# Two thirds of the chunk MLP's u products by seven block products, modulation chapters moved, output parts held behind the next operand's transposes

## The chip, the cores and the metric

The kernel runs on one core of one Trainium2 chip. The metric is the device time of one execution in microseconds (us). TensorE (PE) does the matrix products, VectorE (DVE) and ScalarE (ACT) the elementwise work, GpSimd (POOL) a few small steps, and SyncE (SP) issues nearly all the DMA loads. Each of these engines works through its own list of instructions strictly in the order of that list; an instruction that waits holds up all that stand behind it on its engine.

## The reference

Two layers work on a latent stream x (512 tokens of 1024 channels) and a context (256 tokens). Each layer is a half-step SwiGLU, a token mixer and another SwiGLU; every sub-layer is modulated and post-normalised. Layer 0 mixes with a bidirectional HGRN2, layer 1 with a chunk MLP:

```python
def modulation(cond, w_mod, b_mod):
    m = jax.nn.silu(cond) @ w_mod + b_mod            # nine "chapters" of 1024 per layer
    return m.reshape(m.shape[:-1] + (N_MOD, D_MODEL))
def modulate(x, m, k):
    return x * (1 + m[..., 3 * k + 1, :]) + m[..., 3 * k, :]
def post_norm_update(x, y, m, k, g, b):
    return layer_norm(DN_ALPHA * x + m[..., 3 * k + 2, :] * y, g, b)
def swiglu(h, w_in, w_out):
    gate, up = jnp.split(h @ w_in, 2, axis=-1)
    return (jax.nn.silu(gate) * up) @ w_out           # hidden width 2816
def chunk_mlp(h, n_chunks, w_in, v_g, v_b, w_s, b_s, w_out):
    u, v = jnp.split(jax.nn.gelu(h @ w_in), 2, axis=-1)   # each 3072 wide
    v = layer_norm(v, v_g, v_b)
    v = v.reshape(bsz, n_chunks, CM_CHUNK, CM_GROUPS, CM_INNER // CM_GROUPS)
    v = jnp.einsum('gts,bnsgc->bntgc', w_s, v) + b_s.T[None, None, :, :, None]
    return (u * v.reshape(bsz, length, CM_INNER)) @ w_out
```

So chapters 3k and 3k+1 of a layer (shift and scale) are needed when the operand of sub-layer k is made, and chapter 3k+2 (the gate) when its output is added to x. For layer 1, chapters 6 and 7 belong to the last SwiGLU's input, and chapter 8 is the gate on its output.

## The kernel before, in words

**Precision.** Every large product is made of three fp32r matmuls (lines 148, 149, 150) of operands that are split into a high part (ACT, line 135) and the rest (DVE, line 136). A stationary block is 128x128, a moving block 128 rows by up to 512 tokens.

**Stages on PE.** The first SwiGLU of the latent and context tokens, HGRN2, then f2 (the last SwiGLU of layer 0, up to 1340 us of the profiled execution), f3 (the first of layer 1, up to 1695 us), the chunk MLP and f4, the last SwiGLU. Each SwiGLU has an input phase and an output phase.

**Input phase by seven products (class FeedSums, used by f2, f3 and f4).** The first hidden pairs are made plainly while the operand is still being built (banks named psf); all others come as a gate block and an up block whose 2x2 block product takes seven products of half-size blocks rather than eight: 84 matmuls of 128x256 in banks psc, pse and psa. For that, DVE forms sums of the weights for each pair (lines 594 to 597, from tiles raw and rawu), ACT and DVE split the sums into w, and DVE combines the products (lines 666 to 671). Sums of the operand (f4 to f7) are made once per phase.

**Output phase (class OutPhase).** For each of two column halves, hidden blocks (hs, split from h by lines 135 and 136) are multiplied into four token banks y0 to y3. The last steps of the second half are "held": they run token by token, so that a finished token can be added to x with its gate (line 350), normalised (lines 360 to 374), transposed on PE (pt, line 384) and scaled into the next phase's operand xm while PE still works on later tokens. `run` begins with `self.load_gate(0)`, which loads the gate's row. `finish` scales the residual x by the affine vectors of the norm (lines 343 and 344).

**Chunk MLP.** The v half comes by seven products already, in pairs. The u half is 24 plain units: 24 matmuls of 128x512 per unit into pscu, gelu on ACT (line 1329), then eight short matmuls that mix tokens (pscs, line 1334), then DVE (lines 1341, 1345, 1350). Before the first unit DVE and POOL make the mean and 1/deviation of v (lines 1297 to 1301), and DVE normalises v with them (line 1318).

**Modulation.** One chapter is a queue of nine steps. Eight of them load 512 KB of mod_w and take two dot products of 128x512 on DVE (line 170); the ninth closes the chapter. For a gate chapter the close is a reduction, an addition, a transpose on PE, a copy and a DMA to memory:

```python
nc.vector.reduce_sum(dot, accs[c], axis=AX.X)
if ch % 3 == 2:
    nc.vector.tensor_tensor(dot, dot, mbT[:, l, ch, :], ALU.add)
    pg = bank("pg")
    nc.tensor.transpose(pg[:KD, :P], dot, ident)
```

Other code calls `mod_step(n)` to move the queue on by n steps. `made(key)` runs the queue until that chapter is closed; `load_gate` calls it for the gate:

```python
self.gate = load_row(self.bp, "rgate", made((self.l, 3 * self.j + 2, self.cond))[0, c])
```

In the kernel before, chapters 7, 6 and 8 of layer 1 are queued just ahead of the u stage, are stepped by `mod_step(2)` once in each unit, and are closed well before its end. `Scraps` is a pool that makes the small tiles of a chapter out of one larger tile and takes its weight buffers from the two-buffer ring rawu that the seven products use too.

**What sets the order.** The program text is the order, except where `issue_after` gives work a lower priority: a scheduler then places it among the other work of its engine.

Of the kernel before, what the change touches and what calls it, by code (L numbers as in the profile page):

```python
# [18 lines left out]
P = 128  # L19
# [51 lines left out]
def backbone_kernel(  # L71
# [126 lines left out]
    class Scraps:  # L198


        def __init__(self, pool, small, ring):
            self.pool, self.ring, self.at, self.got = pool, ring, 0, {}
            self.small = pool.tile([P, D], F32, tag=small, name=small, bufs=2)

        def tile(self, shape, dtype, tag, name, bufs=1):
            if tag == "mraw":
                return self.pool.tile(shape, dtype, tag=self.ring, name=self.ring, bufs=2)
            got = self.got.setdefault(tag, [0])
            if got[0] < bufs and tag != "junk" or len(got) == 1:
                got.append(self.at)  # L210
                self.at += int(np.prod(shape[1:]))
                assert self.at <= D
            a = got[1 + got[0] % (len(got) - 1)]
            got[0] += 1
            t = self.small[: shape[0], a : a + int(np.prod(shape[1:]))]
            return t.rearrange("p (k i) -> p k i", i=shape[2]) if len(shape) > 2 else t

    def scraps(sp, l, chs):

        s = sp.tile([P, D], F32, tag="e", name="e", bufs=2)  # L220
# [49 lines left out]
    class OutPhase:  # L270
# [128 lines left out]
        def run(self, bp, hook=None, nmod=0):  # L399
# [27 lines left out]
            self.held.close()  # L427
            if self.release:
                self.release()
            if nxt is not None:  # L430
                nxt.enter()
# [5 lines left out]

            if nxt is None:
                done(0)
                done(1)  # L440
                return
# [157 lines left out]
    class FeedSums(Forms, FeedIn):  # L599


        def __init__(self, l, i, xm, nt, new_block):
            super().__init__(l, i, xm, nt)
            self.place_forms(new_block)

        def rest(self, hp, sp, nmod=0):
            for f in range(len(self.pss) // 2):
# [835 lines left out]
```

## Time and profile before

| | |
|---|---|
| time, median of 3 | 2471.17 us (2470.74 to 2472.19) |
| the profiled execution's own time | 2472.61 us |
| its span on the core | 2470.9 us |
| busy in it: PE, DVE, ACT, POOL | 2426.5, 1919.2, 1133.4, 45.5 us |
| mean granted TensorE clock | 0.996 |

The places that the change touches, by the start of their first PE instruction in the profiled execution:

| us | what starts |
|---|---|
| 984.26, 1340.68, 1694.91, 2108.53 | transposes of the new operand for f2, f3, the chunk MLP, f4 |
| 1017.44, 1371.05, 2138.93 | first pair by seven products of f2, f3, f4 |
| 1822.96 to 1977.06 | u stage of the chunk MLP |
| 1988.75 | main part of its output phase |
| 2341.03 | output phase of f4, the last phase |

Times in the profile are microseconds from the start of the span, means of a group are nanoseconds. A busy interval of a PE row lasts longer than the distance to the next row, since matmuls are pipelined, so PE's pace is read from starts. A row of the windows view gives the stretch, its length, the busy time and number of instructions in it, the granted clock, the DMA share and GB/s.

### The profile page before, as it was taken

Reading aid. Unit: us, or ns where it says so; the run is one execution under the profiler, and the core shown is the slowest. Engines: PE = TensorE matmul, PEld = TensorE weight load, DVE = VectorE, ACT = ScalarE, POOL = GpSimd, SP = SyncE. Lnnn points to the kernel's source line nnn. Section 1 sums busy time; section 2 is a strip of 40 time slices with the busy share of each in tenths; the row PEclk is TensorE's granted clock in tenths of the full one; section 3 lists DMA queues with packets and bytes.
Section 4 is the critical chain, followed back from the end, with each engine's and each line's share of the span. In section 5 each row is a group of like instructions: output and inputs, shape, how many; then the busy total and the mean of one; then the engine's idle time right before and its main releaser. Section 6 shows DMA issues by size and latency. Waiting matters only on the chain.

```text
span 2470.9 us, 37394 instructions
## 1 busy us (share of the span) xinstructions
PE 2426.5 (98%) x14619; PEld 2181.9 (88%) x14619; DVE 1919.2 (78%) x3426; ACT 1133.4 (46%) x1726; POOL 45.5 (2%) x83
## 2 busy tenths in 40 slices
PE   7999999999999999999999999999999999999998
PEld 5888889987888888999988999988988888999986
DVE  7965679685588886998886988887889466998765
ACT  4222344453454552655643555544652243555641
POOL 0000000000000000000000000000000000000001
PEclk9999999999999999999999999999999999999999
DMA  8866555874211214332463333673356243332332
GB/s 318 297 204 200 166 196 186 287 250 139 69 60 52 60 52 159 111 128 104 151 216 129 111 104 109 205 221 129 103 186 221 86 149 115 128 125 103 103 113 71
DMA packets 106851, 365.45 MB, mean 148 GB/s; under 512 B 12409, under 2 KB 13617, under 8 KB 106673
## 3 DMA queue, kind: packets, MB, share of 16 engines
q1 hardware_dynamic: 106672, 363.06, 44.3%
q8 instruction: 114, 1.87, 0.3%
q14 instruction: 65, 0.52, 0.1%
HBM read 350.40 MB, written 12.61 MB: 147 GB/s over the span
## 4 chain that ended last, share of the span: by engine, by line
PE 83%; DVE 11%; ACT 2%; issue 2%; DMA 1%; POOL 1%; SPq 0%; POOLq 0%; DVEq 0%; ACTq 0%
PE y L150 8%; PE y L149 8%; PE y L148 8%; PE psf L149 6%; PE psf L150 6%; PE psf L148 6%; PE psc L148 5%; PE psc L150 5%; PE psc L149 5%; PE pse L148 2%; PE pse L150 2%; PE pse L149 2%; PE pscu L148 2%; PE pscu L149 2%; PE pscu L150 2%
## 5 line engine op out<-in xcount | busy, mean ns | idle before, releaser
L136 DVE TENSOR_TENSOR w<-raw,w 128x1024 fp32r<-128x1024 f32 (+2 forms) x446 | 505.3, 1136 | 150.6 <-ACT w L135 149.6
L135 ACT ACTIVATE w<-raw 128x1024 fp32r<-128x1024 f32 (+2 forms) x446 | 439.5, 987 | 352.5 <-PE y L150 91.7
L150 PE MATMUL y<-w,hs 128*128 128x512 f32 x984 | 383.3, 390 | 0.8 <-DVE hs L136 0.8
L148 PE MATMUL y<-w,hs 128*128 128x512 f32 x984 | 383.4, 390 | 0.6 <-ACT hs L135 0.6
L149 PE MATMUL y<-w,hs 128*128 128x512 f32 x984 | 382.9, 389 | 0.0
L135 ACT ACTIVATE hs<-h 128x512 fp32r<-128x512 f32 (+1 forms) x220 | 127.2, 588 | 232.5 <-PE y L150 216.7
L150 PEld LDWEIGHTS y<-w,hs 128*128 128x128 f32 x984 | 184.7, 188 | 40.7 <-DVE hs L136 2.5
L148 PEld LDWEIGHTS y<-w,hs 128*128 128x128 f32 x984 | 184.7, 188 | 39.4 <-ACT hs L135 1.0
L149 PEld LDWEIGHTS y<-w,hs 128*128 128x128 f32 x984 | 184.7, 188 | 38.3
L148 PE MATMUL psf<-xm,w 128*128 128x512 f32 (+1 forms) x544 | 192.9, 361 | 17.5 <-ACT xm L135 17.2
L136 DVE TENSOR_TENSOR hs<-h,hs 128x512 fp32r<-128x512 f32 (+1 forms) x220 | 135.6, 634 | 93.7 <-ACT hs L135 93.6
L150 PE MATMUL psf<-xm,w 128*128 128x512 f32 (+1 forms) x544 | 194.2, 358 | 2.3 <-DVE w L136 2.3
L149 PE MATMUL psf<-xm,w 128*128 128x512 f32 (+1 forms) x544 | 194.5, 358 | 0.7 <-DVE xm L136 0.5
L148 PE MATMUL pse<-f,w 128*128 128x256 f32 x480 | 136.2, 284 | 3.3 <-ACT w L135 3.3
L148 PE MATMUL psc<-f,w 128*128 128x256 f32 x480 | 136.1, 284 | 0.0
L148 PE MATMUL psc<-xm,w 128*128 128x256 f32 x480 | 135.9, 283 | 0.0
L150 PE MATMUL pse<-f,w 128*128 128x256 f32 x480 | 135.9, 283 | 0.0
L149 PE MATMUL pse<-f,w 128*128 128x256 f32 x480 | 135.8, 283 | 0.0
L149 PE MATMUL psc<-xm,w 128*128 128x256 f32 x480 | 135.8, 283 | 0.0
L149 PE MATMUL psc<-f,w 128*128 128x256 f32 x480 | 135.8, 283 | 0.0
L150 PE MATMUL psc<-f,w 128*128 128x256 f32 x480 | 135.8, 283 | 0.0
L150 PE MATMUL psc<-xm,w 128*128 128x256 f32 x480 | 135.8, 283 | 0.0
(314 smaller groups left out, 6006.3 us busy)
## 6 DMA issues: line engine op xcount, KB each, us to landing
raw<-in_ffn_w_in SPq DMA_DIRECT2D x160, 512.0 KB, 4.4
raw<-in_ffn_w_out SPq DMA_DIRECT2D x110, 512.0 KB, 4.0
mraw<-in_mod_w SPq DMA_DIRECT2D x104, 512.0 KB, 4.3
rawu<-in_ffn_w_in SPq DMA_DIRECT2D x60, 512.0 KB, 3.5
rawu<-in_mod_w SPq DMA_DIRECT2D x40, 512.0 KB, 4.4
x<-x SPq DMA_DIRECT2D x36, 512.0 KB, 4.2
raw<-in_hg_wf SPq DMA_DIRECT2D x32, 512.0 KB, 3.5
raw<-in_cm_wu SPq DMA_DIRECT2D x24, 512.0 KB, 4.0
```

The source lines that it names most:

```text
L135: nc.scalar.activation(dst_hi, src, AF.Copy)
L136: latest[0] = nc.vector.tensor_tensor(dst_lo, src, dst_hi.bitcast(F32), ALU.subtract)
L148: nc.tensor.matmul(ps, ah, bh, start=start, stop=False, **kw)
L149: nc.tensor.matmul(ps, ah, bl, start=False, stop=False, **kw)
L150: return nc.tensor.matmul(ps, al, bh, start=False, stop=stop, **kw)
```

## The change

1. In the u stage, `seven` (moved out of FeedSums into a class that both users share) makes two units together by seven products, for 16 of the 24 units; the other 8 stay plain. The units are taken in pairs, the operand's sums stay until the last pair, and DVE normalises each group of v just ahead of its use.
2. Chapters 7 and 6 move from the u stage into the chunk MLP's output phase, one step per loop step. Chapter 8 moves to the last phase: it is queued by `scraps(sp, 1, (8,))` just ahead of `op.run`.
3. In an output phase that leads into another phase and has more than two blocks of tokens (the five that end at about 380, 984, 1341, 1695 and 2109 us), the last token's last two held steps (12 matmuls) are issued behind the transposes of the first two blocks of the next operand. What followed the held parts moves with them, and the second pair of tokens is staged into psf one block later.
4. In the first pair of FeedSums, one product (psa) comes right behind the first one, and the last product gets a bank of its own (psb).
5. The scaling of x in `finish` is given a lower priority.

```diff
-    def scraps(sp, l, chs):
+    def scraps(sp, l, chs, small=None):
...
-        small = Scraps(sp, "e", "rawu")
+        small = Scraps(sp, small, "rawu")
...
-                for x in self.xs:
-                    nc.vector.scalar_tensor_tensor(x[:, c], x[:, c], ALPHA, g, ALU.mult, ALU.mult)
-                    nc.vector.scalar_tensor_tensor(x[:, c], b, ALPHA, x[:, c], ALU.mult, ALU.add)
+                with tc.issue_after(latest[0].ins):
+                    for x in self.xs:
+                        nc.vector.scalar_tensor_tensor(x[:, c], x[:, c], ALPHA, g, ALU.mult, ALU.mult)
+                        nc.vector.scalar_tensor_tensor(x[:, c], b, ALPHA, x[:, c], ALU.mult, ALU.add)
...
+            back = 2 if nxt is not None and nt > 2 else 0
+            rest = [(1, *h, [nt - 1]) for h in held[len(held) - back :]]
             for t in range(nt):
-                for h in held:
+                for h in held[: len(held) - back * (t == nt - 1)]:
                     self.part(1, *h, [t])
...
             for i in range(len(steps) + 3):
-                if i == 1 and nt > 2:
-                    done(1)
+                if i == back:
+                    for r in rest:
+                        self.part(*r)
+                    close()
+                    nxt.enter()
+                    if nt > 2:
+                        done(1)
                 if i:
                     nxt.ahead(i)
+                if back and i == 4:
+                    nxt.staged(*steps[1])
                 if i < len(steps):
-                    last = self.operand(*steps[i])
-                if i >= 3:
-                    nxt.staged(*steps[i - 3])
+                    self.operand(*steps[i])
+                j = i - 2 if back and i > 3 else i - 3
+                if 0 <= j < len(steps):
+                    nxt.staged(*steps[j])
...
+            product(pc, wg, 0, b11, True, True)
+            kept(0, pc)
+            if early:
                 product(pa, wg, K2, b21, True, True)
+            product(pe, we, 0, self.f5, True, True)
...
-            modp = early.enter_context(swap("modp3"))
-            srow = {"x": silu_row(modp, "x")}
-            for ch in (7, 6, 8):
-                queue_mod(modp, srow, 1, ch, ["x"])
...
+            def by_sums(j):
+                u0, u1 = (cu.tile([P, T], F32, tag="u", name="u", bufs=4) for _ in range(2))
+                sc = cu.tile([P, 2 * P], F32, tag="sc3", name="sc3", bufs=1)
+                lo, hi = slice(0, 2 * P), slice(2 * P, T)
+                pa, pe, pc, _ = gin.seven(xm, sp, cm_wu[j], cm_wu[j + 1], [u0[:, lo], u1[:, hi], u1[:, lo], sc])
...
+            for j in range(0, 3 * NG, 2):
+                for i in (j, j + 1):
+                    if i % 3 == 0:
+                        normalize(i // 3)
+                        hs.append(vhp.tile([P, 3, T], F32, tag="vh", name="ht"))
+                if j % 6 < 4:
+                    us = by_sums(j)
+                else:
+                    us = plain(j), plain(j + 1)
...
-                    mod_step(2)
...
-        op.run(bp)
+        small = vhp.tile([P, NT, GC], F32, tag="vh", name="vt").rearrange("p t c -> p (t c)")
+        scraps(modp, 1, (7, 6), small)
+        op.run(bp, None, 1)
...
         op.affine = (1, 1)
-        op.run(bp)
+        scraps(sp, 1, (8,))
+        op.run(bp, None, 1)
```

How the instructions move at three places. First, PE at the passage from the chunk MLP's output phase to f4, before and then now. y3 is the last token's bank, pt the transposes of the new operand's blocks from the normalised x of the first tokens, psf the first plain product of f4; each y3 row stands for itself and the two rows of its three matmuls that are left out.

```order
L148 MATMUL y3_19472<-w_19801,hs_19807 128x512
...
L148 MATMUL y3_19472<-w_19812,hs_19815 128x512
...
L148 MATMUL y3_19472<-w_19812,hs_19818 128x512
...
L384 MATMUL pt_19947<-ident_74,x_19065 128x128
...
L384 MATMUL pt_19979<-ident_74,x_19065 128x128
...
L384 MATMUL pt_19989<-ident_74,x_19065 128x128
...
L148 MATMUL psf_20009<-xm_19056,w_19827 128x256
```

```order
L148 MATMUL y3_19811<-w_20156,hs_20162 128x512
...
L390 MATMUL pt_20293<-ident_74,x_19361 128x128
...
L390 MATMUL pt_20303<-ident_74,x_19361 128x128
...
L148 MATMUL y3_19811<-w_20167,hs_20170 128x512
...
L148 MATMUL y3_19811<-w_20178,hs_20184 128x512
...
L390 MATMUL pt_20356<-ident_74,x_19361 128x128
...
L148 MATMUL psf_20376<-xm_19349,w_20193 128x256
```

The last 12 matmuls of y3 now stand between the transposes of the second and third block, ahead of psf.

Second, PE at the passage from the last pair by seven products (psc) to the output phase of f4 (y0), before and then now. pg is the transpose that closes chapter 8.

```order
L148 MATMUL psc_22614<-xm_19056,w_22611 128x256
L149 MATMUL psc_22614<-xm_19056,w_22611 128x256
L150 MATMUL psc_22614<-xm_19056,w_22611 128x256
L148 MATMUL y0_22729<-w_22735,hs_22741 128x512
L149 MATMUL y0_22729<-w_22735,hs_22741 128x512
L150 MATMUL y0_22729<-w_22735,hs_22741 128x512
```

```order
L148 MATMUL psc_22986<-xm_19349,w_22983 128x256
L149 MATMUL psc_22986<-xm_19349,w_22983 128x256
L150 MATMUL psc_22986<-xm_19349,w_22983 128x256
L187 MATMUL pg_23122<-ident_74,e_23085 8x128
L148 MATMUL y0_23141<-w_23147,hs_23153 128x512
L149 MATMUL y0_23141<-w_23147,hs_23153 128x512
```

A gate's transpose now stands between the last pair and the first product of the last phase; in the kernel before it stood in the u stage.

Third, DVE at the same place, before and then now. silu, h: the last pair is combined. hs: the hidden blocks' low parts for the last phase. L170: dots of chapter 8, with rawu as the buffers its weights are loaded into. L349, L350: the scaling of x. L183 and L185: the reduction and the addition that close the chapter.

```order
L666 TENSOR_TENSOR silu_22706<-psa_22616,sc_22617 128x256
L136 TENSOR_TENSOR w_22867<-raw_22865,w_22867 128x1024
L668 TENSOR_TENSOR h_22707<-sc_22617 128x256
L669 TENSOR_TENSOR h_22707<-pse_22615,sc_22617 128x256
L136 TENSOR_TENSOR hs_22741<-h_20288,hs_22741 128x512
L136 TENSOR_TENSOR hs_22744<-h_20292,hs_22744 128x512
L136 TENSOR_TENSOR hs_22776<-h_20408,hs_22776 128x512
```

```order
L170 SCALAR_TENSOR_TENSOR e_23085<-rawu_23100,e_23084 128x512
L710 TENSOR_TENSOR h_22964<-pse_22987,sc_22962 128x256
...
L136 TENSOR_TENSOR hs_23153<-h_20655,hs_23153 128x512
...
L170 SCALAR_TENSOR_TENSOR e_23085<-rawu_23104,e_23084 128x512
...
L170 SCALAR_TENSOR_TENSOR e_23085<-rawu_23108,e_23084 128x512
...
L349 SCALAR_TENSOR_TENSOR x_23129<-x_23129,rg_23253 128x512
...
L170 SCALAR_TENSOR_TENSOR e_23085<-rawu_23112,e_23084 128x512
...
L170 SCALAR_TENSOR_TENSOR e_23085<-rawu_23116,e_23084 128x512
...
L183 TENSOR_REDUCE e_23085<-e_23085 128x8
...
L185 TENSOR_TENSOR e_23085<-e_23085,mbT_81 128x8
```

From the combination of the last pair (h from pse) to L185, 26 rows of DVE's list now follow each other: h from pse itself and the product of h and silu, nine dots, six of hs, seven of the scaling of x, the reduction and the addition; the two dots of rawu_23100 stand around the first of them.

More of the change, by code (lines that the diff above doesn't have):

```diff
@@ L638, in operands @@
                 return wg, we, wu, weights(g, K2)
-            first = len(self.hs)
-            for f in range(first, NF):
-                if f == first:
-                    with tc.issue_after(self.summed.ins):
-                        wg, we, wu, w4 = operands(f)
-                else:
-                    wg, we, wu, w4 = operands(f)
-                pc, pe, pa = bank("psc"), bank("pse"), bank("psa")
-                sc = sp.tile([P, 4, N2], F32, tag="sc", name="sc", bufs=2)
-                def kept(i, ps, scale=1.0):
-                    nc.scalar.activation(sc[:, i, :], ps[:, :N2], AF.Copy, scale=scale)
-                product(pc, wg, 0, b11, True, True)
-                kept(0, pc)
-                product(pe, we, 0, self.f5, True, True)
-                kept(1, pe)
-                product(pc, we, K2, self.f6, False, True)
-                kept(2, pc)
-                product(pa, wg, K2, b21, True, True)
+            if after is not None:
+                with tc.issue_after(after.ins):
+                    wg, we, wu, w4 = operands()
+            else:
+                wg, we, wu, w4 = operands()
@@ L664, in rest @@
                 s = hp.tile([P, T], F32, tag="silu", name="silu", bufs=1)
                 h = hp.tile([P, T], F32, tag="h", name="h", bufs=NF)
-                nc.vector.tensor_tensor(s[:, :N2], pa[:, :N2], sc[:, 0, :], ALU.add)
+                pa, pe, pc, pb = self.seven(
+                    self.xm, sp, self.src(2 * f), self.src(2 * f + 1), [sc[:, i, :] for i in range(4)],
+                    self.summed if f == first else None, f == first,
+                )
+                if pb is not None:
+                    nc.vector.tensor_tensor(s[:, N2:], sc[:, 3, :], pb, ALU.subtract)
```

164 lines of the change are left out of this document (100 added, 64 removed).

## The prediction

> **What bounds the kernel now.** I read the page's busy times and chain first, then TensorE by stage, then its waits.
>
> ```profile
> PE 2426.5 (98%) x14619; PEld 2181.9 (88%) x14619; DVE 1919.2 (78%) x3426; ACT 1133.4 (46%) x1726; POOL 45.5 (2%) x83
> PE 83%; DVE 11%; ACT 2%; issue 2%; DMA 1%; POOL 1%; SPq 0%; POOLq 0%; DVEq 0%; ACTq 0%
> ```
>
> TensorE is the bound: time falls only by fewer matmul columns or by shorter waits of PE, and any wait put at PE's head is paid in full. The windows view of PE, cut at the stages (stretch, length, busy, count, granted clock, DMA):
>
> ```profile
> 1220.96:1340.68 119.72, 119.72 (x531) 1.00 0.54 178
> 1340.68:1371.05 30.37, 28.51 (x226) 0.94 0.40 131
> ...
> 1822.96:1977.06 154.10, 152.28 (x763) 1.00 0.53 172
> ...
> 2108.53:2138.93 30.40, 28.54 (x225) 0.94 0.31 108
> 2138.93:2341.03 202.10, 202.10 (x1682) 1.00 0.34 116
> ```
>
> Rows 1, 3 and 5 (f2's output phase, the u stage, the pairs of f4) hold hardly any idle time. Rows 2 and 4, the passages into f3 and f4, have idle time and a lower clock. What PE waits for (total, times, longest; then single windows):
>
> ```profile
> PE psf L148 <- ACT xm L135: 17.2, 4, 12.8
> PE pse L148 <- ACT w L135: 3.3, 2, 1.9
> ...
> PE pt L384 <- DVE x L374: 2.4, 1, 2.4
> ...
> PE pscs L1334 <- DVE vt L1318: 1.8, 1, 1.8
> PE pscv L148 <- ACT xm L135: 1.7, 1, 1.7
> ```
>
> ```profile
> PE pt L384 <- DVE x L374: 2.4, 1, 2.4
> ...
> PE psf L148 <- ACT xm L135: 0.7, 1, 0.7
> ```
>
> ```profile
> PE psf L148 <- ACT xm L135: 1.8, 1, 1.8
> ```
>
> The two windows are the passages into f2 and into f4; f3's wait is of f4's size. 12.8 of the 17.2 us is the program's start, which stays. The clock behind these waits:
>
> ```profile
> 987.60:994.40 6.80, 5.99 (x27) 0.50 0.54 202
> ...
> 1346.00:1349.40 3.40, 3.40 (x19) 0.50 0.91 320
> 2114.00:2117.40 3.40, 3.40 (x18) 0.50 0.41 152
> ```
>
> A wait of 1.8 us at f3 and f4 is followed by 3.4 us at half clock, 1.7 us lost; f2's 2.4 us wait by 6.8 us, 3.4 lost.
>
> **The change, part by part.** *The u stage.* Pace from starts of consecutive rows:
>
> ```profile
> 1905.98 0.39 PE L149 MATMUL pscu<-xm,w 128*128 128x512 f32 x1
> 1906.20 0.39 PE L150 MATMUL pscu<-xm,w 128*128 128x512 f32 x1
> ...
> 1907.11 1.05 PE L1334 MATMUL pscs<-wsT,vt 128*128 128x128 f32 x8
> 1908.00 0.27 PE L187 MATMUL pg<-ident,dot 128*8 128x128 f32 x1
> 1908.03 0.47 PE L148 MATMUL pscu<-xm,w 128*128 128x512 f32 x1
> ```
>
> 1905.98 to 1907.11 is five matmuls, 0.227 us each, so a plain pair of units costs 48 x 0.227 = 10.9 us. A pair by seven products is the f4 row: 202.10 / 20 = 10.1 us. Eight pairs: -6.2. (By columns one eighth of 10.9 should go, 1.36; the smaller matmuls keep 0.8 of it.) The 1.8 us wait of pscs for the normalised v goes too, since two units' products now stand ahead of the first pscs.
>
> Against that, the first pair needs sums. DVE's first aggregation of v's statistics:
>
> ```profile
> 1821.31 0.81 DVE L1297 BATCH_NORM_AGGREGATE cmv<-cst 128x2 f32<-128x48 f32 x3
> ```
>
> Behind the last statistics DVE must make four sums (0.61 each), the normalising of a group (four of 0.4), four statistics and their ends (about 0.5 each) and a 1.14 us split, 7.2 us, from about 1821.3 on: the first sum's weights are ready near 1828.5. PE has psc and psa to do from 1823, 24 matmuls of 0.12 us, till 1825.9. That is a wait of 2.6; since the products are interleaved in two pieces I take 3.5, bounds 0 (statistics give way) and 5. Stage: -6.2 - 1.8 + 3.5 = -4.5. DVE as a whole is not the limit there:
>
> ```profile
> 1822.96:1977.06 154.10, 113.89 (x242) 1.00 0.53 172
> 1220.96:1340.68 119.72, 89.75 (x163) 1.00 0.54 178
> ```
>
> These are DVE's rows. In the u stage it leaves 40 us, and 48 dots of 0.61 us (29 us) leave; a summed pair adds four sums (2.4), 1.7 of splits and 1.0 of combining, 8 x 5.1 = 41. That is 126 of 146 us: it fits, on average.
>
> *Chapters 7 and 6.* 32 dots, 32 x 0.61 = 20 us, enter an output phase of 131 us. The second row is f2's output phase, which carries chapters in the same manner, with PE busy 119.72 of 119.72: cost 0. The cover is the phase's own length; without it, each late hs costs about a dot, 0.6 us.
>
> *Held parts.* 12 matmuls x 0.227 = 2.7 us now stand between the first transposes and psf, where PE waits 1.7 to 1.8 us at f3, the chunk MLP and f4. They cover it, and with it f3's and f4's half clock: gains of 3.5, 1.7, 3.5. At f2 the long wait is pt for x, ahead of the held parts, so only 0.7 us goes. But the second pair of tokens is staged a block later, 24 matmuls x 0.12 = 2.9 us, and the sums for the first seven-product pair stand behind it on DVE. The psa product put forward covers 1.4. Where pse waits already (f2 and f3, the 3.3 us row) up to 1.4 more is lost; at f4, which waits for nothing there, I count 2. Net: f2 +0.5, f3 -2.9, chunk MLP -1.3, f4 -1.5, sum -5.2; bounds -9.4 (no pair later) and 0 (all of it later). The scaling of x costs DVE what it did; ahead of PE's work it is nowhere.
>
> *Chapter 8.* Here is the largest term. `load_gate(0)` opens the last phase and calls `made` for chapter 8, whose close is a PE transpose. In the kernel before it is the pg row above: it ran between two units, 0.03 us of PE, because its last dot lay 7 us back:
>
> ```profile
> L170 DVE SCALAR_TENSOR_TENSOR junk<-mraw,srow_x x176: 628/685/693, 55.4 to 1900.1; 128x512 bf16<-128x512 f32 x176
> ```
>
> Now pg stands ahead of y0's first matmul, and everything of the last phase is queued behind it on PE. It waits for L185, and that for the 26 DVE rows. Where DVE is at that place before (its timeline, and PE's first row):
>
> ```profile
> 2336.84 1.23 DVE L136 TENSOR_TENSOR w<-raw,w 128x1024 fp32r<-128x1024 f32 x1 [3.07 <-ACT w L135]
> ...
> 2338.32 1.22 DVE L136 TENSOR_TENSOR w<-raw,w 128x1024 fp32r<-128x1024 f32 x1
> 2339.45 0.42 DVE L668 TENSOR_TENSOR h<-sc 128x256 f32<-128x256 f32 x1
> 2339.80 0.42 DVE L669 TENSOR_TENSOR h<-pse,sc 128x256 f32<-128x256 f32 x1
> 2340.14 1.88 DVE L136 TENSOR_TENSOR hs<-h,hs 128x512 fp32r<-128x512 f32 x3
> 2341.94 0.68 DVE L671 TENSOR_TENSOR h<-h,silu 128x512 f32<-128x512 f32 x1
> ```
>
> ```profile
> 2341.03 0.40 PE L148 MATMUL y<-w,hs 128*128 128x512 f32 x1
> ```
>
> And the pace of dots among hs, from f2's output phase:
>
> ```profile
> 1223.09 1.29 DVE L136 TENSOR_TENSOR hs<-h,hs 128x512 fp32r<-128x512 f32 x2
> 1224.30 0.68 DVE L170 SCALAR_TENSOR_TENSOR e<-rawu,e 128x512 f32<-128x512 f32 x1
> ...
> 1224.91 0.69 DVE L136 TENSOR_TENSOR hs<-h,hs 128x512 fp32r<-128x512 f32 x1
> ```
>
> Each 512-element row takes 0.605 us from start to start. In the old clock: h from pse at 2339.80, a dot ahead of it, 2340.41; then 0.34 for it, 23 rows of 512 (nine dots, six hs, seven scalings, one product) at 0.605, 13.9, and some 0.3 for the two small rows: 2354.95. PE would have begun at 2341.03: a wait of 13.9, with the transpose itself (0.27) and the way there 14.4 us. It cannot be much less, as PE has nothing else it may do. It can be more, by the weights. Four of the eight loads go out only after DVE has freed one of two buffers:
>
> ```profile
> rawu<-in_mod_w SPq DMA_DIRECT2D x40, 512.0 KB, 4.4
> ```
>
> Dots of load 6 end near +7.1, load 8 lands 4.4 later at +11.5, while DVE gets to it at +10.7: 0.8 more, so 15 us; at 6.5 us each it would be 19. If DVE is ahead by part of the slack that it had (the 3.07 us idle ahead of the first row), 12. I take 14.4. After so long a wait the clock is at half: by the rows above 3.4 to 6.8 us, 1.7 to 3.4 lost, taken 2.6. SP's order past its loads of w costs nothing while PE stands.
>
> *Sum.* -4.5 - 5.2 + 14.4 + 2.6 = +7.3. New first-pair waits of 2 to 3.5 us (u stage, f2, f3, f4) can each bring a half-clock stretch, 1.7; bounds 0 and 6.8, taken 0.9. Together +8.2 on the profiled 2472.61, 2480.8; this execution lies 1.4 above the median, so 2471.17 + 8.2 = 2479.4 us.
>
> [...]
>
> **Rivals.** *Gains cancel the loss.* Held parts at their bound (-9.4), no first-pair wait in the u stage (-8.0), the gate wait 14.4 + 1.7: -1.3, so 2470, no change. For it: the passages' waits are all in the rows above. Against: it needs DVE to be early at each passage, where two of three already wait for w.
>
> *Faster, because the gate's transpose comes early.* If the dots ran mostly ahead of T, as before's idle DVE near the end would allow, the wait would be under 4 us, and the sum 4 - 9.7 = -6: 2465. It decides the sign below about 9 us of wait. Against: nine dots and seven scalings stand behind h from pse in DVE's list, which itself can't run before the last products.
>
> *DVE becomes the bound.* In the u stage 126 of 146 us is an average; in DVE's list the summed pairs carry the sums and the plain ones do not, so a summed pair alone takes 12 to 13 us of DVE with its spatial part, more than its 10.1 + 1.8 on PE. If that decides, the stage gains nothing (+5), and loads at 6.5 us make the gate wait 19 (+5): 2489. For it: pse waits for w already at two passages. Against: in f4 DVE carries 20 pairs without one wait.
>
> **How the numbers follow.** This kernel's measurement can tell about 0.2% (5 us) from no change: faster is below 2466.2, slower above 2476.1. The forecast (2473 to 2485) gets 0.50, of which 0.06 lies within 0.2%; DVE as bound 0.16; cancelled gains 0.24; early transpose 0.10. So slower 0.60, same 0.30, faster 0.10. Range: 2466 to 2488, down to the edge of the early transpose, up to the loads' bound; the likeliest case's own range is 2473 to 2485.
>
> **What would show it.** At the start of the last phase, one PE wait of 12 to 19 us, pg for DVE L185, with half clock behind it; none would prove the largest term wrong. The passages into f3 and f4 without the wait of psf for xm and at clock 1.0; pse waiting for w there 1 to 3 us. The u stage, 12 pairs in about 150 us, with one wait of pse of some 3 us at its start and then none; more waits of pse would speak for DVE as the bound. The chunk MLP's output phase without PE idle time. If the gains at passages and u stage together exceed 15 us, I am wrong on the sign of what is left.

## The result, and the profile after

The changed kernel takes 2492.95 us (median of 4 runs, 2487.88 to 2494.43), the kernel before 2471.68 us beside it (2470.74 to 2472.8): the ratio is 1.0082, 95% interval 1.0065 to 1.01. The sign of the forecast was right, its size was not: +21 us in place of +8, above the range of 2466 to 2488. The profiled execution of the changed kernel took 2491.97 us with a span of 2490.3 us, 19.4 more than the 2470.9 of before; the accounts below are made between these two spans.

The page of the changed kernel, busy times and chain by engine:

```profile
PE 2424.8 (97%) x14907; PEld 2193.0 (88%) x14907; DVE 1964.6 (79%) x3501; ACT 1154.6 (46%) x1781; POOL 43.7 (2%) x83
PE 80%; DVE 12%; ACT 3%; DMA 2%; issue 2%; POOL 1%; SPq 0%; POOLq 0%; DVEq 0%; ACTq 0%
```

PE's busy time fell by 1.7 us; the time that was added is time in which PE stood. Its waits (total, times, longest):

```profile
PE pg L187 <- DVE e L185: 15.3, 1, 15.3
PE psf L148 <- ACT xm L135: 13.0, 2, 12.6
PE pse L148 <- ACT w L135: 7.4, 4, 2.4
PE pt L390 <- DVE x L380: 5.7, 5, 2.0
...
PE pse L150 <- DVE w L136: 2.3, 1, 2.3
PE psb L148 <- ACT w L135: 2.1, 3, 0.7
```

The first row is the gate's transpose. The second says that the waits of psf for xm at f3 and f4 are gone. The others are new or longer: pse and psb wait for the first weights' sums, at f2, f3, f4 (2.4 and 0.7 us each) and in the u stage (2.3), and the transposes wait for x (5.7 us in all, 2.4 before). The windows view of PE, two passages, their pairs, the u stage, and the last phase from pg on:

```profile
1341.05:1370.62 29.57, 29.49 (x237) 1.00 0.43 151
1370.62:1578.54 207.92, 204.92 (x1682) 0.98 0.34 112
1825.58:1976.65 151.07, 148.48 (x1054) 0.99 0.32 101
2107.15:2136.73 29.58, 29.46 (x237) 1.00 0.25 89
2136.73:2343.43 206.70, 203.62 (x1682) 0.99 0.38 127
2358.91:2362.90 3.99, 3.99 (x10) 0.50 0.34 117
2358.91:2490.30 131.39, 121.91 (x529) 0.97 0.29 92
```

The passages hold 12 matmuls more than before (2.7 us) and are 0.8 us shorter, without idle time and at full clock: there the held parts do what was expected. But the pairs behind them take 207.9 and 206.7 us where the same rows of before had 204.0 and 202.1. Behind each of the four first pairs the clock is at half:

```profile
1025.00:1028.37 3.37, 3.37 (x18) 0.50 0.46 157
1376.54:1383.36 6.82, 6.17 (x29) 0.50 0.45 154
1833.92:1837.33 3.41, 3.41 (x18) 0.50 0.80 268
2144.53:2147.94 3.41, 3.41 (x19) 0.50 0.56 180
```

17.0 us at half clock, 8.5 lost. Put together by stretches of PE's timeline, from the start of the first row of a stretch to that of the next (us; before, after, difference):

| stretch | before | after | difference |
|---|---|---|---|
| start to HGRN's output phase (holds the passage at 380 us) | 956.70 | 958.03 | +1.3 |
| HGRN's output phase and the passage into f2 | 60.74 | 59.30 | -1.4 |
| pairs of f2 | 203.52 | 206.73 | +3.2 |
| f2's output phase and the passage into f3 | 150.09 | 146.56 | -3.5 |
| pairs of f3 | 203.99 | 207.92 | +3.9 |
| f3's output phase, passage into the chunk MLP, its v half | 246.61 | 247.04 | +0.4 |
| u stage | 155.41 | 151.07 | -4.3 |
| chunk MLP's output phase and the passage into f4 | 161.87 | 160.08 | -1.8 |
| pairs of f4 | 202.10 | 206.70 | +4.6 |
| wait of the gate's transpose | 0 | 15.5 | +15.5 |
| the last phase from there | 129.87 | 131.39 | +1.5 |

The gate's wait in detail, on DVE and then PE:

```profile
2343.68 0.69 DVE L170 SCALAR_TENSOR_TENSOR e<-rawu,e 128x512 bf16<-128x512 f32 x1 [1.42 <-DMA rawu<-in_mod_w]
...
2344.30 0.42 DVE L710 TENSOR_TENSOR h<-pse,sc 128x256 f32<-128x256 f32 x1
...
2345.24 0.68 DVE L136 TENSOR_TENSOR hs<-h,hs 128x512 fp32r<-128x512 f32 x1
...
2356.80 0.68 DVE L170 SCALAR_TENSOR_TENSOR e<-rawu,e 128x512 bf16<-128x512 f32 x1
...
2358.70 0.15 DVE L185 TENSOR_TENSOR e<-e,mbT 128x8 f32<-128x8 f32 x1
```

```profile
2358.91 0.37 PE L187 MATMUL pg<-ident,e 128*8 128x128 f32 x1 [15.33 <-DVE e L185]
```

The first hs, which the last phase begins with, was split by 2345.9, 13 us before PE could use it. From h<-pse to L185 DVE took 14.4 us (14.5 had been worked out); just ahead of that DVE had waited 1.4 us for one load of mod_w.

### The profile page after: what moved, and what is told of

The parts are those of the page before. It is cut to its first block, busy times and chain, and to the rows that moved or that the text cites. A ratio compares the mean times of both kernels' runs of the same rounds, so it can differ in the third digit from the quotient of the medians.

```text
span 2490.3 us, 38139 instructions
## 1 busy us (share of the span) xinstructions
PE 2424.8 (97%) x14907; PEld 2193.0 (88%) x14907; DVE 1964.6 (79%) x3501; ACT 1154.6 (46%) x1781; POOL 43.7 (2%) x83
## 4 chain that ended last, share of the span: by engine, by line
PE 80%; DVE 12%; ACT 3%; DMA 2%; issue 2%; POOL 1%; SPq 0%; POOLq 0%; DVEq 0%; ACTq 0%
PE y L150 8%; PE y L148 8%; PE y L149 8%; PE psf L149 5%; PE psf L150 5%; PE psf L148 5%; PE psc L150 5%; PE psc L148 5%; PE psc L149 5%; PE pse L150 3%; PE pse L148 3%; PE pse L149 3%; DVE w L136 1%; PE psa L149 1%; PE psa L150 1%
## 5 line engine op out<-in xcount | busy, mean ns | idle before, releaser
L148 PE MATMUL pse<-f,w 128*128 128x256 f32 x544 | 155.6, 286 | 7.4 <-ACT w L135 7.4
L150 PE MATMUL pse<-f,w 128*128 128x256 f32 x544 | 155.4, 286 | 2.3 <-DVE w L136 2.3
L150 PE MATMUL psc<-f,w 128*128 128x256 f32 x544 | 156.0, 287 | 0.0
L149 PE MATMUL psc<-f,w 128*128 128x256 f32 x544 | 155.7, 286 | 0.0
L148 PE MATMUL psc<-f,w 128*128 128x256 f32 x544 | 155.6, 286 | 0.0
L149 PE MATMUL pse<-f,w 128*128 128x256 f32 x544 | 155.1, 285 | 0.0
L148 PE MATMUL psc<-xm,w 128*128 128x256 f32 x532 | 151.6, 285 | 0.0
L150 PE MATMUL psc<-xm,w 128*128 128x256 f32 x532 | 150.6, 283 | 0.0
L149 PE MATMUL psc<-xm,w 128*128 128x256 f32 x532 | 150.6, 283 | 0.0
```

The costliest lines, as they stand in the source:

```text
L148: nc.tensor.matmul(ps, ah, bh, start=start, stop=False, **kw)
L149: nc.tensor.matmul(ps, ah, bl, start=False, stop=False, **kw)
L150: return nc.tensor.matmul(ps, al, bh, start=False, stop=stop, **kw)
```

## The experiments

Each kernel was timed in five rounds beside the kernel before. The columns: median, range and runs, ratio to before with its 95% interval.

| kernel | us | ratio |
|---|---|---|
| e1 late gate | 2472.63 (2471.88 to 2475.53, 11) | 1.0006 (0.9997 to 1.0015) |
| e2 e1, old held parts and staging | 2464.56 (2461.0 to 2469.12, 9) | 0.9971 (0.9962 to 0.9981) |
| e3 e1, old order of the first pair | 2476.31 (2474.14 to 2478.83, 11) | 1.0019 (1.001 to 1.0028) |
| e4 e1, all of u plain | 2475.28 (2474.12 to 2480.78, 11) | 1.0017 (1.0008 to 1.0026) |
| e5 e1, one held step | 2475.92 (2472.46 to 2480.05, 11) | 1.001 (1.0001 to 1.002) |
| e6 e1, third token's norm earlier | 2472.84 (2468.04 to 2475.45, 11) | 0.9999 (0.999 to 1.0008) |
| e7 e2, u begun by a plain pair | 2461.19 (2460.98 to 2461.78, 5) | 0.9956 (0.9943 to 0.9969) |
| e8 e2, old order of the first pair | 2463.11 (2461.82 to 2466.09, 5) | 0.9966 (0.9953 to 0.9979) |
| e9 e1, a plain pair more in f2 to f4 | 2464.21 (2463.42 to 2467.38, 7) | 0.997 (0.996 to 0.9981) |
| e10 e7, the same | 2464.43 (2462.87 to 2467.95, 7) | 0.997 (0.9959 to 0.998) |
| e11 e9, u begun by a plain pair | 2461.3 (2460.58 to 2462.45, 5) | 0.9956 (0.9943 to 0.997) |
| e12 before, finish at lower priority | 2467.09 (2465.82 to 2470.83, 11) | 0.9981 (0.9972 to 0.999) |
| e13 e1, old staging only | 2459.68 (2457.8 to 2461.84, 5) | 0.9949 (0.9935 to 0.9963) |
| e14 e2, changed staging only | 2478.43 (2473.07 to 2481.85, 11) | 1.0024 (1.0016 to 1.0033) |
| e15 e7, old order of the first pair | 2460.23 (2459.8 to 2462.43, 5) | 0.9953 (0.994 to 0.9965) |
| e16 e13, u begun by a plain pair | 2457.73 (2455.98 to 2459.23, 5) | 0.9943 (0.9929 to 0.9956) |

### The gate asked for late

```diff
-            self.load_gate(0)
+            if self.nxt is not None:
+                self.load_gate(0)
...
             self.lead(0, self.npair, nmod)
+            if self.nxt is None:
+                self.load_gate(0)
             for t in range(nt):
                 self.evac(0, t)
```

> The changed kernel with one thing moved: in the last phase the gate of chapter 8 is asked for behind the first half's products instead of ahead of them, so the chapter's dots are stepped through that half and its transpose stands some 216 matmuls (49 us) into the phase. Theory (the transpose at PE's head costs its wait of 15.3 us and the 1.5 us by which the rest of the phase grew at half clock): 17 us less than the changed kernel, 2476 us. Rival (the last phase is bound by something else, DVE or the loads of mod_w, and the wait only shows there): less than 6 us back, 2487 or more, with a new wait of y for hs.

2472.63, 20 us less than the changed kernel's 2492.95. pg's wait is gone and no wait of y for hs took its place; the last phase starts at 2341.46 and ends the span at 2470.9, 129.4 us, as before. 17 us of the 20 are the expected wait and half clock; between the two profiled executions 2 us more are gone, 1.1 of them in the pairs of f3, where 3.4 us are at half clock in place of 6.8. The theory holds, and what remains is that the rest of the change gains nothing: e1 and before are equal.

### Held parts and staging undone together

```diff
-            back = 2 if nxt is not None and nt > 2 else 0
+            back = 0
...
+            close()
+            nxt.enter()
             nxt.ahead(0)
             done(0)
...
-                if i == back:
-                    for r in rest:
-                        self.part(*r)
-                    close()
-                    nxt.enter()
-                    if nt > 2:
-                        done(1)
+                if i == 1 and nt > 2:
+                    done(1)
```

With back at 0 the staging is the old one as well.

> The kernel with the late gate, and the held parts put back as before: all of the last token's held products ahead of the new operand's transposes, the second pair of tokens staged as early as before. Theory (the later staging makes the first pair of seven products wait 3.4 us in f2, f3 and f4, with half clock behind each, and this costs more than the covered waits of psf gain): 5 to 10 us faster than the kernel with the late gate, 2466 to 2471. Rival (the first pairs wait because of their new order of products, not because of the staging): the wait of pse stays at 2.3 us in f2, f3 and f4, and since the waits of psf for xm come back the time is 3 to 7 us longer, 2479 to 2483.

2464.56, 8 us less than e1. PE's waits, its first rows:

```profile
PE psf L148 <- ACT xm L135: 18.1, 4, 12.6
PE pt L390 <- DVE x L380: 2.9, 2, 2.5
...
PE pse L150 <- DVE w L136: 2.3, 1, 2.3
```

psf waits for xm again, and pse and psb no longer wait at f2, f3 and f4; the 2.3 us left are the u stage's. So this part of the change, meant for the waits of psf, costs 8 us as it stands.

### The order within the first pair

```diff
-                    self.summed if f == first else None, f == first,
+                    self.summed if f == first else None, False,
```

> The kernel with the late gate, and the first pair of f2, f3 and f4 with its products in the order of the other pairs and no bank of its own for the last product. Theory (the order covers 1.44 us of the wait): each of the three waits of pse grows from 2.4 to about 3.8 us and the 0.7 us waits of psb go, 2 us more in all plus any further half clock, 2476 to 2482. Rival (the early order is what makes the first pair slow, the bank psb waiting for w): 3 us or more faster than the kernel with the late gate.

2476.31, 3.7 more than e1; the row of pse:

```profile
PE pse L148 <- ACT w L135: 11.7, 4, 3.8
```

3.8 where it was 2.4: the psa product ahead covers its 1.44 us of pse, of which some comes back at psb. All waits of pse and psb together are 14.4 us here and 11.4 in e1, so the order is worth 1 us of wait in each first pair. Where there is no wait, it is worth nothing:

> The kernel with the late gate and the old held parts, with the first pair's products in the order of the other pairs. Theory (with the old held parts the order psa-first covers the 1.4 and 1.9 us that pse waited at f2 and f3 in the kernel before): pse waits 1.2 to 1.9 us at f2 and f3 and nothing at f4, 2 to 5 us over 2464.6. Rival (the waits went with the scaling of x at lower priority, not with the order): no such wait, within 1.5 us of 2464.6.

e8 was 2463.11 against 2464.56, with waits of pse of 0.4 us or less at the first pairs of f2, f3 and f4. The rival won: with the old held parts the waits that f2 and f3 had before (1.4 and 1.9) went with something else than the order. What it was, e12 below shows. e15 repeats the same edit on e7:

> The fastest kernel so far (late gate, old held parts, u stage begun plainly, 2461.2) with the first pair's products in the order of the other pairs. With the old held parts that order was worth -1.4 us here (2463.1 against 2464.6). If that holds: 2459 to 2461. If it was the spread of the clock: 2461 to 2463.

2460.23 against 2461.19, inside the first expectation; the ranges overlap and it stays open whether that is more than the spread.

### The u stage

e4 replaces the choice `if j % 6 < 4:` by `if False:`, e7 by `if j % 6 >= 2:`.

> The kernel with the late gate, and all 24 units of the u stage made plainly; the moved chapters and the held parts stay. Theory (eight pairs save 0.78 us each, the first sums cost 2.6 us of wait and a half-clock stretch of 1.7): 2 us more than the kernel with the late gate, 2478, with a u stage of about 153 us. Rival (DVE's sums also cost time later, in the chunk MLP's output phase): the time is the same or less than with the late gate, and the wait of y for hs in that output phase is gone.

> The kernel with the late gate and the old held parts (2464.6), with the plain pair of each group of six units put first rather than last, so that the u stage begins with a plain pair; still 16 of 24 units by seven products. Theory (the first sums stand behind v's statistics on DVE, and a plain pair of 10.9 us covers them): the 2.3 us wait of pse and the half-clock stretch of 1.7 us behind it go, 2460 to 2462; a wait of pscs for vt of up to 1.8 us may come back. Rival (it is the loads of rawu that are late, or DVE as a whole): a wait of pse of the same size at the second pair, no gain.

2475.28, 2.65 more than e1, and 2461.19, 3.4 less than e2. The stage from its first pw to the output phase, in PE's windows of e4, e2 and e7:

```profile
1824.24:1977.15 152.91, 152.91 (x765) 1.00 0.30 97
```

```profile
1817.74:1968.64 150.90, 148.31 (x1054) 0.99 0.32 101
```

```profile
1817.56:1965.30 147.74, 146.95 (x1053) 1.00 0.27 84
```

All plain 152.9, seven products first 150.9, a plain pair first 147.7. In the second row 2.6 us are idle and one stretch of 3.4 us is at half clock; in the third 0.8 us are idle, nothing is at half clock, and no wait of pscs for vt came back. A plain pair ahead would also cover late loads, so the run alone does not tell the two causes apart. DVE's rows in the changed kernel do: the first four sums (L612 to L615, 1824.39 to 1829.39) stand between rows of v's statistics and normalisation, and none of them waits for a load. So the first sums stood behind v's statistics on DVE. Eight pairs by seven products save 5.2 us, of which the changed kernel kept 1.8 (its stage is 151.1).

### What makes the first sums late

Two runs asked whether it is the last two tokens' normalisation, which the changed loop issues a step later. e5 sets `back = 1`; e6 moves one token's part:

```diff
+                if back and i == 1:
+                    self.evac(1, 2)
+                    self.norm(2)
                 if i == back:
...
-                    if nt > 2:
-                        done(1)
+                    if back:
+                        self.evac(1, 3)
+                        self.norm(3)
+                    elif nt > 2:
+                        done(1)
```

> The kernel with the late gate, with one held step (6 matmuls, 1.4 us) behind the first transposes instead of two, so that the last two tokens are added and normalised one loop step earlier, as before; the order of staging stays the changed one. Theory A (the first pair is late because the last two tokens' normalisation is issued a step later): pse at the first pairs of f2, f3 and f4 waits 1 us or less, time 5 to 8 us under the late gate's 2472.6, 2465 to 2468. Theory B (it is late because of the changed staging order): the waits stay at 2.3 us, time within 2 us of 2472.6.

> The kernel with the late gate, both held steps behind the transposes, but of the last two tokens the one that is complete already is added and normalised a loop step earlier; only the last token's work stays behind the held products. Theory A (lateness of the last two tokens' normalisation): about half of the wait goes, pse 1 to 1.5 us at f2, f3, f4, psf without a wait for xm, time 3 to 6 us under 2472.6. Theory B (staging order): no change of the waits, within 2 us of 2472.6.

2475.92 and 2472.84 against 2472.63: in both, pse waits 7.4 us in all, as in e1. Theory A fell. e5 is 3.3 us slower than e1, which theory B did not expect either, and the cause of that stays open. Then two runs gave PE a plain pair to do in that time (e9 with the held parts as changed, e10 on the kernel without them):

```diff
+            f, pss = len(self.hs), []
+            for u in range(2):
+                w = unit(self.src(2 * f + u))
+                ps = bank("psf")
+                feat_mm(ps, w, self.xm, 0, self.n)
+                pss.append(ps)
+            self.evac(hp, *pss)
             N2, first = 2 * P, len(self.hs)
```

> The kernel with the late gate and the held parts as changed; in f2, f3 and f4 one more hidden pair is made plainly (10.9 us of products that need no sums) ahead of the first pair by seven products. Theory (the held parts do bring PE 3.5 us sooner to the first pair, but the weights' sums hang on DVE's own chain behind the last two tokens, which is no shorter, so PE waits the gain away and then runs at half clock): no wait of pse or psb at f2, f3, f4 and no half clock behind them; 3 x 3.4 of waits and about 6 of half clock go, 3 x 0.8 for the plain pairs comes, 2458 to 2463. Rival (the sums are late for another reason, the loads or the order within the pair): the waits of 2.3 us move behind the plain pair, 2474 or more.

> The kernel with the late gate, the old held parts and the u stage begun plainly (2461.2), with the same extra plain pair in f2, f3 and f4. There is no wait of pse there to be covered. Theory: 3 x 0.8 = 2.4 us slower, 2463 to 2464, the half clock behind psf as in that kernel. Rival (a plain pair also gives DVE room that pays later): not slower than 2461.2.

> Late gate, held parts as changed, the extra plain pair in f2, f3 and f4, and the u stage begun plainly. Theory: the 4 us that the plain start of the u stage saved come on top of the kernel with held parts and plain pairs, 2454 to 2460, under the 2461.2 of the kernel with the old held parts. Rival (the held parts are worth nothing even with their wait covered): 2463 or more.

e9 took 2464.21, 1 us over its range; pse and psb no longer wait in f2 to f4 and the half clock behind them is gone, so the waits are for DVE's sums and the cover works. e10 took 2464.43, 3.2 over e7 (2.4 were expected). e11 took 2461.3, 1.3 over its range and level with e7, but 3.1 under e10, which differs from it in the held parts and their staging alone: with the wait covered these gain about what the plain pairs cost (3.2).

That left the staging order. e13 undoes it alone, e14 does it alone:

```diff
-                if back and i == 4:
-                    nxt.staged(*steps[1])
...
-                j = i - 2 if back and i > 3 else i - 3
+                j = i - 3
```

> The kernel with the late gate and both held steps behind the first transposes, with the old order of staging: the first block of the second pair of tokens is transposed ahead of the second psf block of the first pair. Theory B (the staging order makes DVE's sums late): the waits of pse at f2, f3 and f4 fall to 1 us or less, 2464 to 2468. Theory C (the sums hang on the last two tokens' chain through DVE, whatever is staged, and PE only comes earlier): PE waits as long in all, now for x at the transposes of the second pair (1.5 us or more in each passage) in place of part of the wait of pse; within 3 us of 2472.6.

> The kernel with the late gate and the old held parts (2464.6), with the changed order of staging alone. Theory B: the first transposes of the second pair come 2.9 us later with nothing gained, and pse waits 1.5 to 3 us at f2, f3 and f4: 2470 to 2478. Theory C: the last two tokens' chain is behind by less than the 2.9 us, pse waits under 1.5 us, 2464 to 2468.

2459.68 and 2478.43: 13 us less than e1, and 14 more than e2. Theory B holds in both, with sizes beyond what it expected (2464 to 2468; 2470 to 2478). PE's waits in the passage into f4 and its first pair, e14 first, e13 second:

```profile
PE pse L148 <- ACT w L135: 2.4, 1, 2.4
PE psf L148 <- ACT xm L135: 1.8, 1, 1.8
PE psb L148 <- ACT w L135: 0.7, 1, 0.7
```

```profile
PE pt L390 <- DVE x L380: 1.0, 1, 1.0
```

With the old staging the held parts do their work: no psf wait, no pse wait, 1.0 us for x. Four kernels differ in these two parts of the change alone:

| | old staging | changed staging |
|---|---|---|
| old held parts | 2464.56 (e2) | 2478.43 (e14) |
| held parts as changed | 2459.68 (e13) | 2472.63 (e1) |

The changed staging costs 13.9 us with the old held parts and 13.0 with the changed ones; the changed held parts gain 4.9 and 5.8. The two effects add. So the wait of pse does not come from PE being early through the held parts, as the theory of e9 had it: e14 leaves them out and waits as long. PE's rows at the passage into f4 show what it comes from: the last transposes of the operand, the first row of the first pair, and its first pse, in the changed kernel, e14 and e13:

```profile
2127.66 0.60 PE L390 MATMUL pt<-ident,x 128*128 128x128 f32 x4
...
2136.73 0.28 PE L148 MATMUL psc<-xm,w 128*128 128x256 f32 x1
...
2142.12 0.39 PE L148 MATMUL pse<-f,w 128*128 128x256 f32 x1 [2.35 <-ACT w L135]
```

```profile
2129.87 0.60 PE L390 MATMUL pt<-ident,x 128*128 128x128 f32 x4
...
2138.94 0.28 PE L148 MATMUL psc<-xm,w 128*128 128x256 f32 x1
...
2144.33 0.38 PE L148 MATMUL pse<-f,w 128*128 128x256 f32 x1 [2.35 <-ACT w L135]
```

```profile
2114.99 0.60 PE L390 MATMUL pt<-ident,x 128*128 128x128 f32 x4
...
2126.94 0.28 PE L148 MATMUL psc<-xm,w 128*128 128x256 f32 x1
...
2129.82 0.28 PE L148 MATMUL pse<-f,w 128*128 128x256 f32 x1
```

Behind the last transposes PE has 9.07 us of work before the first pair in the two kernels with the changed order (72 matmuls of psf) and 11.95 us in e13 (96): one block of 24, 2.88 us, now stands ahead of the transposes. The first sums' weights come 14.46 us behind the last transposes in the changed kernel and in e14 alike, and PE waits for them; in e13 PE itself gets to pse only 14.83 us behind them and does not wait. So the block that was put ahead of the transposes is work that PE no longer has while DVE and ACT go from these transposes to the first weights, and it comes back as a wait, 2.4 at pse and 0.7 at psb.

### finish at lower priority, alone

The edit to the kernel before is the one to `finish` in the diff of the change, and nothing else.

> The kernel before with one part of the change alone: the scaling of x in finish at lower priority. Theory (several of its rows, 0.6 us each, stood in DVE's chain from the transposes of f2 and f3 to the first weights' sums, about 3 us in each; without them the waits of pse there, 1.4 and 1.9 us, go): 3 to 6 us faster than before, 2466 to 2469, no wait of pse at f2 and f3. Rival (as the prediction had it, the place of these rows costs nothing; the waits went for another reason): within 1.5 us of before, the waits of pse unchanged.

2467.09, 4.85 less than before beside it. The waits of pse at f2 and f3 went. In the kernel before, rows of that scaling stood in DVE's chain of f3; its timeline, first and last of the five between 1350 and 1367 us:

```profile
1350.38 0.68 DVE L343 SCALAR_TENSOR_TENSOR x<-x,rg 128x512 f32<-128x512 f32 x1
...
1366.74 0.68 DVE L343 SCALAR_TENSOR_TENSOR x<-x,rg 128x512 f32<-128x512 f32 x1
```

Five of 0.6 us, 3 us ahead of the first sums. In the changed kernel line 349 first runs at 1230.8 us, behind the passage into f2, and none of these rows runs in the passage into f3 (1335 to 1380 us). Between the two profiled executions the waits of pse are 3.3 us less, that of psf at f2 1.0 more, and 6.8 us fewer are at half clock (3.4 lost), half of them at f2 and half behind psf at f4. Such stretches come and go (the mean granted clock of e12's executions lies between 0.996 and 0.998), so it is not shown that all of the 4.85 us belongs to these rows.

### The causes put together

e16 is e13 with the u stage begun by a plain pair.

> Late gate, held parts as changed, the old order of staging (2459.7), and the u stage begun with a plain pair. Theory: the two gains are in different stages and add, so the 2.3 us wait of pse at the head of the u stage and the half clock behind it go here too: 2455 to 2458, the fastest of all kernels. Rival (the wait moves to pscs for vt, or the clock's gain was chance): 2459 or more.

2457.73, 2 under e13 and 0.57% faster than before (ratio 0.9943, 0.9929 to 0.9956). Two small moves away from the changed kernel's worst places (the gate's close, the staging) and one in the u stage turn +21 us into -14. Its lead over e13 is smaller than the 3.4 us that the same edit gave on e2, and the two ranges overlap.

## Why the prediction was right and wrong

**Chapter 8: right, and the largest term.** Forecast 14.4 us of wait for pg and 2.6 for the clock behind it; measured 15.5 and 1.5, and e1 takes it away. That both add up to 17.0 is partly luck, since the two misses cancel. Of the bounds for late loads, 0.8 to 4.6 us, 1.4 came about. The half clock was there for 4.0 us behind pg. The trace of before alone would not have shown it: it lies in the order of PE's new list.

**The u stage: right in its sum.** Forecast -4.5, measured -4.3. Its parts were each off by up to 1 us and cancel in part: the stage with all units plain (e4) is 2.5 shorter than before (forecast 1.8, the wait of pscs), the eight pairs save 5.2 (forecast 6.2), the wait of the first sums was 2.6 (forecast 3.5), and a half-clock stretch of 1.7 came with it that was counted elsewhere. The claim that DVE carries the rest held: no later wait of pse in the stage.

**Held parts and their staging: wrong, and the step that failed.** The prediction had for the passages f2 +0.5, f3 -2.9, chunk MLP -1.3, f4 -1.5, and 0.9 for half clock behind first pairs: -4.3. Measured over the table's rows outside the u stage and the last phase: +6.7, 11 us more. In the terms of the sum:

- The step that failed is the price of the later staging: "up to 1.4 more is lost; at f4, which waits for nothing there, I count 2". Its mechanism was right (the second pair of tokens staged a block later, 2.9 us, DVE's sums behind it). Its size was not: the net figures of the passages hold 4.2 us for it (9.4 of gains less 5.2), and the runs show 13.0 (e1 against e13) and 13.9 (e14 against e2). The 1.44 us of psa was taken off the 2.9; in the runs the order of psa was worth 1 us of wait in a pair (e3), and the waits were still 2.4 and 0.7 at each of f2, f3 and f4, 9.2 us in all. The rest is half clock in the main: 5.1 us more was lost to it in e14's profiled execution than in e2's.
- That half clock was taken at 0.9 of a range of 0 to 6.8. It came in all four places, once for 6.8 us: 8.5 lost, above the range's end. The prediction saw that 1.8 us of wait had 3.4 us at half clock behind it in the rows of before and did not draw the conclusion for waits of 2.3.
- The gain of the held parts was counted too large: 9.4 at its full size, 4.9 and 5.8 in the runs. The waits of 1.8 at f3 and f4 came down to 0.9 and 1.0 for x with the old staging (e13), and the half clock that was counted behind both came behind only 7 of the 16 such waits in the traces here.
- At the passage at 380 us there was no wait to cover, and the transposes, which now come earlier, wait 1.1 us for x (+1.3 in its row). Into the chunk MLP the wait of pscv for xm went from 1.7 to 0.4 us, and the transposes wait 1.1 there (+0.4 in its row).
- "The scaling of x ... is nowhere" was wrong with the sign in the change's favour: e12 has it at -4.85. Without it the changed kernel would have been slower still.

**Chapters 7 and 6: nearly right.** Forecast 0; one wait of y for hs of 1.3 us in the chunk MLP's output phase (1.5 in e1). e4, which has the same chapters there and makes u plainly, waits 0.5, so the chapters alone are not the whole cause.

**The clock behind the waits.** The 0.9 rested on rows of before, where each of the two waits of 1.8 us at f3 and f4 has 3.4 us at half clock behind it. In the runs, waits of pse of 2.3 us and more (the longest 3.8) had half clock beside or behind them in four of four first pairs of the changed kernel, and in 27 of 31 over the traces of all kernels here; the waits of psf of 1.8 us at f3 and f4 had it in 7 of 16. At the first pairs of the changed kernel the stretches lasted 3.4 us three times and 6.8 us once. The longest, 17.07 us (2345.83 to 2362.90), began in the wait for pg; its last 3.99 us lie behind pg. The rows of before pointed the right way and should have had more weight.

**The rivals.** None happened. DVE did not become the bound of the u stage, the transpose did not come early, and the gains did not cancel the loss; but e1 shows that without the gate's wait the gains and losses of the rest cancel to nothing.

## What to carry to other kernels

Work that is stepped along in the background has an end that may need another engine; before moving it, look where that last instruction lands in the other engine's list, for here a transpose of 0.3 us at the head of a phase held up all that stood behind it for 15.3 us. Before work of the bounding engine is moved ahead of the row from which another engine starts its chain, count what the bounding engine still has to do between that row and the result it needs: here a block of 2.9 us moved out of that stretch came back as waits of 2.4 and 0.7 us. Parts of a change that can be told apart should be priced and tried apart: here the held parts were worth 5 us and the order of staging beside them cost 13, and together they looked like one idea that costs 8. A short wait also has a price behind it when the clock falls: here 1.7 us for each 3.4 us at half clock, behind waits of 2.3 and 2.4 us.

## What the runs showed of the hardware

In the changed kernel each wait of 2.3 to 2.4 us at a first pair was followed by 3.4 us at half clock, at f3 by 6.8. Over all kernels it was 27 of 31 waits of pse of 2.3 us and more (not, for one, 2.4 us at f2 in e4). Waits of 1.8 us of psf at f3 and f4 did so in 7 of 16 cases (e7 at f4: yes, e2 at f3 and f4: no).

Executions of one kernel here lie up to 9 us apart (e14), against 2 us in the four of the kernel before beside the changed one. The mean granted clock of each execution goes with it: in e14 it was 0.996 in the two fastest (2473.07 and 2475.1) and 0.992 in the slowest (2481.85), and 0.004 of 2475 us is 9.9 us. What makes the clock differ between executions of one kernel was not tested.
